# A decoder layer on one core: the bias strip table built from 17 copies, score operands and pool splits ordered behind other DVE work

## The chip, the cores and the metric

The kernel runs on one core of a Trainium2 chip. The time is device microseconds of one execution on that core; smaller is better. The kernel before was timed three times: 660.46, 660.73 and 663.38 us, median 660.73. One more execution was profiled, and all traces here come from it.

## What is computed

One decoder layer over 512 tokens of width 1024, in float32. The parts that matter here are the input projection, the attention branch and the pooling branch:

```python
proj = h @ w_in[l]
q, k, v, p, g = jnp.split(proj, [512, 1024, 1536, 2048], axis=-1)
y_attn = moba_attention(q, k, v, rel_bias) @ w_branch_attn[l]      # 8 heads x 64, causal
y_pool = multiscale_pool(p, w_pool_group[l], pool_scale[l]) @ w_branch_pool[l]
gates = sigmoid(g).reshape(B, S, 2, D)
mixed = gates[:, :, 0] * y_attn + gates[:, :, 1] * y_pool
h = layer_norm(ALPHA * h + mixed @ w_out[l], ln1_g[l], ln1_b[l])
...
```

In the attention a bias `rel_bias[head, bucket(q_pos - k_pos)]` is added to each score, and later keys are masked with -1e30. The bucket is the distance itself up to 15, then grows with its logarithm, to 31 for every distance from 113 on. So along the distances 0 to 511 there are 32 runs of equal buckets: 16 of length 1, then 16 of lengths 2 to 14 and one of 399. The pooling branch takes causal means over windows of 2, 4, 8 and 16 tokens of four groups of 128 channels, and multiplies each group with a small matrix. Behind the part shown follow a gated MLP with a short convolution and a second layer norm; the change does not touch them.

## The kernel before

**Arithmetic.** Each float32 matrix is split into a rounded part `hi` and a rest `lo`; `split` (L65) makes `hi` with one ACT copy and `lo` with one DVE subtraction, and `mm3` (L210) sums three matmuls, hi by hi, hi by lo and lo by hi. Weights come in tiles of 128x1024: a DMA issued by SP into `wraw`, a split into a ring of five `whi`/`wlo` pairs, then the matmuls. `weights(i)` fetches up to three tiles ahead.

**`seven`** (L245) computes two 128-column tiles of a product over all tokens with seven block products in place of eight. It works on four weight combinations: `A` (one tile as it is, loaded as `araw`), `X` (a difference formed in the load: SP writes one tile's part, then POOL adds the other with an accumulating DMA, L163 and L164), `D` (half a tile) and `Y` (formed from `X` and `A` by two DVE additions, L174). The token side uses four combinations `T` made beforehand by `t_form` (L230). Results are put together by ACT copies (L253, L257, L259) and DVE additions: L261, L265, then L266, which writes the first half of the bank in which the last block product, `Y` part 1, goes on. That last block product and the call of `done` are left in `pending` and run inside the next `seven` (or by `flush`), behind its second group of matmuls.

**The order of the start.** The value projection (`v`), two plain pool tiles (`p`, j = 2 and 3), then `seven` for product 0 (pool tiles 0 and 1) and for products 1 to 4 (query tile and key tile of head pairs 0 to 3). `pool_in` (L407) makes window sums with POOL additions (L416) and finishes them on DVE (L419 to L421, and a split into `difs`). `heads_done` (L457) copies a finished query tile to `raw_q` with ACT (L459); for pair 0 it calls `heads(0)` at once.

**`heads(p)`** (L403) makes the score operands of a head pair from `raw_q` and `raw_k`: for each of the two heads one `q` tile (an ACT instruction, L385, and a DVE instruction, L386) and a `k` and a `kl` tile (two ACT, L397, and two DVE, L398). That is six instructions of ACT and six of DVE for a pair. Three buffers each hold the `q`, `k` and `kl` tiles.

**The attention stage.** `scores(h)` (L490) asks for the bias strip of head h+2, multiplies (L501, L502), adds the strip and takes row maxima on DVE (L505), negates them (`nm`, L508), takes exponentials on ACT (L511), and scales on POOL (L516). `trans` transposes on TensorE (L530), `pv` multiplies with the values (L543). The loop over the heads puts one gate tile (`in_tile`, 24 matmuls of 512 columns) into each step. From head 4 on it also splits one of four `zT` tiles, which the pooling half of the branch products reads after the stage.

**The strip table.** Scores of one head need a 128x512 strip whose row shifts by one per partition. POOL builds one row of 640 floats per head in `F_sb` (8 partitions): a memset of the last 128 to -1e30 (L342) and one copy per run of equal buckets from the small table `rel`, 32 copies (L347). A DMA writes the rows to `F_d` in DRAM (L349), and `load_strip` (L351, L353) reads a strip back with overlapping rows. `F_sb` lies in one of the two buffers of the tag `dif`; the strips share three buffers of the tag `strip`, the first of which starts out as `wg_raw`.

**What sets the order.** Every engine runs its instructions in the order that a planner gave them. The planner walks through a simulated execution, and what comes first in the program text has priority among what is ready; work far down in the text is taken early when an engine has nothing else. `tc.issue_after(ins)` makes the instructions of its block come behind `ins` on the engine of `ins`, without waiting for its result.

Of the kernel before, what the change touches and what calls it, by code (L numbers as in the profile page):

```python
# [8 lines left out]
F32 = mybir.dt.float32  # L9
F32R = mybir.dt.float32r  # L10
AF = mybir.ActivationFunctionType
ALU = mybir.AluOpType
PSUM = bass.MemoryType.PSUM

P = 128
S = 512
# [3 lines left out]
H = 8  # L20
# [8 lines left out]
NEG = -1e30  # L29
STRIP = 640  # L30
# [15 lines left out]
def layer_kernel(ctx: ExitStack, tc: tile.TileContext, xT, x, w_v, w_c, rel_bias, invcnt, w_group,  # L46
                 pscale, w_br, w_out, lnr, w_fi, convp, w_fo, out):
    nc = tc.nc
# [16 lines left out]
    def split(hi, lo, src, copy=None):  # L65
        if copy:
            copy(hi, src)
        else:
            nc.scalar.activation(hi, src, AF.Copy)  # L69
        return nc.vector.tensor_tensor(lo, src, hi.bitcast(F32), op=ALU.subtract)  # L70
# [42 lines left out]
    state = {"next": 0, "limit": WO0 - 1}  # L113
# [107 lines left out]
    t1, t2 = slice(0, 256), slice(256, 512)  # L221
# [23 lines left out]
    def seven(key, whole, tt, y, u, done, between=None):  # L245
        ba, bb, bc = (bank(f"s{q}{key[0]}{key[1]}") for q in "abc")
        chain, low, c11 = ba[:, 256:], bb[:, :256], bc[:, :256]

        def b_(k, t):
            return whole[0][:, k, t], whole[1][:, k, t]  # L250

        s_mm(key, "A", 0, b_(k1, t1), chain, True)
        nc.scalar.activation(y, chain, AF.Copy)  # L253
        s_mm(key, "A", 1, b_(k2, t1), c11, True)
        flush()
        s_mm(key, "X", 0, tt["T3"], low, True)
        nc.scalar.activation(u[:, t2], low, AF.Copy)  # L257
        s_mm(key, "Y", 0, tt["nT2"], chain, False)
        nc.scalar.activation(u[:, t1], chain, AF.Copy)  # L259
        s_mm(key, "D", 0, tt["T4"], low, False)  # L260
        nc.vector.tensor_tensor(u[:, t1], u[:, t1], low, op=ALU.add)  # L261
        if between:
            between()
        s_mm(key, "X", 1, tt["nT1"], chain, False, between)
        nc.vector.tensor_tensor(u[:, t2], u[:, t2], chain, op=ALU.add)  # L265
        nc.vector.tensor_tensor(ba[:, t1], y, c11, op=ALU.add)  # L266

        def close():
            s_mm(key, "Y", 1, b_(k2, t2), chain, False, between)
            done(ba, u)  # L270

        pending.append(close)
# [12 lines left out]
    zT = keepp.enter_context(tc.tile_pool(name="keepz", bufs=1)).tile([P, 4, S], F32, name="zT")  # L285
    attn = ExitStack()
    av = attn.enter_context(tc.tile_pool(name="av", bufs=3, side="right", reuse_waits="tile"))
# [5 lines left out]
    ti = {n: tuple(pw.tile([P, 4, 256], F32R, name=f"i{n}_{q}") for q in ("hi", "lo")) for n in parts}  # L293
    pw.tile([P, 48], F32, name="pw_gap2")
    xr = [pw.tile([P, 4, S], F32, name=f"xr{n}") for n in range(2)]
    F_sb = pw.tile([H, STRIP], F32, tag="dif", name="F_sb", bufs=2)

    eps_t = const.tile([P, 1], F32, name="eps_t")
    nc.gpsimd.memset(eps_t, EPS)
# [22 lines left out]
    behind = ExitStack()  # L322
# [16 lines left out]

    behind.close()  # L340
    F_d = dram.tile([H, STRIP], F32, name="F_d")
    nc.gpsimd.memset(F_sb[:, S:], NEG)  # L342
    lo_ = 0
    for b, n in _bucket_runs():
        e = F_sb[:, S - lo_ - n:S - lo_]
        (pst, pn), _ = rel.ap
        nc.gpsimd.tensor_copy(e, bass.AP(tensor=rel.tensor, offset=rel.offset + b, ap=[[pst, pn], [0, n]]))  # L347
        lo_ += n
    nc.gpsimd.dma_start(F_d, F_sb)  # L349

    def load_strip(h):  # L351
        strips[h] = av.tile([P, S], F32, tag="strip", name=f"strip{h}")
        nc.gpsimd.dma_start(strips[h], bass.AP(tensor=F_d.tensor, offset=F_d.offset + h * STRIP,  # L353
                                               ap=[[1, P], [1, S]]))

    load_strip(0)
    load_strip(1)

    vv = av.tile([P, NT, H * DH], F32, name="vv", bufs=1)
    bs = [bank(f"v{j}") for j in range(NT)]  # L360
# [15 lines left out]
    dif = {}  # L376
# [4 lines left out]
    def q_done(p, b):  # L381
        for e in range(2):
            own, oth = slice(e * DH, (e + 1) * DH), slice((1 - e) * DH, (2 - e) * DH)
            t = av.tile([P, S], F32R, tag="q1", name=f"q1_{2 * p + e}")
            nc.scalar.activation(flip(t[own, :]), b[own, :], AF.Copy, scale=DH ** -0.5)  # L385
            nc.vector.scalar_tensor_tensor(flip(t[oth, :]), b[own, :], DH ** -0.5, flip(t[own, :]).bitcast(F32),  # L386
                                           op0=ALU.mult, op1=ALU.subtract)
            Q1[2 * p + e] = t


    def k_done(p, b):
        for e in range(2):
            own, oth = slice(e * DH, (e + 1) * DH), slice((1 - e) * DH, (2 - e) * DH)
            hi = av.tile([P, S], F32R, tag="k1", name=f"k1_{2 * p + e}")
            lo = av.tile([P, S], F32R, tag="kl", name=f"kl_{2 * p + e}")
            for half in (own, oth):
                nc.scalar.activation(hi[half, :], b[own, :], AF.Copy, scale=-1.0)  # L397
                nc.vector.scalar_tensor_tensor(lo[half, :], b[own, :], -1.0, hi[own, :].bitcast(F32),  # L398
                                               op0=ALU.mult, op1=ALU.subtract)
            K1[2 * p + e] = hi  # L400
            KL[2 * p + e] = lo

    def heads(p):  # L403
        q_done(p, raw_q[p])
        k_done(p, raw_k[p])

    def pool_in(j, b, sign=1.0):  # L407
        w = POOL_WINDOWS[j]
# [17 lines left out]
    def pool_out(j):  # L426
        b = bank(f"zb{j}")
        mm3(b, (wg_hi[:, j, :], wg_lo[:, j, :]), dif[j], True, True)
        nc.scalar.activation(zT[:, j, :], b, AF.Copy, scale=psc[:, j:j + 1])
# [20 lines left out]
    raw_q = {}  # L450
# [5 lines left out]

    def heads_done(p, ba):  # L457
        raw_q[p] = av.tile([P, S], F32, tag="rq", name=f"rq{p}")
        nc.scalar.activation(raw_q[p], ba, AF.Copy)  # L459
        if p == 0:  # L460
            heads(0)

    for n in range(1 + pairs):
        if n == 0:
            u, done = xr[1][:, 3, :], pool_done
        else:
            u = raw_k[n - 1] = av.tile([P, S], F32, tag="rk", name=f"rk{n - 1}")
            done = lambda ba, u, p=n - 1: heads_done(p, ba)
        seven(("i", n), (xT_hi, xT_lo), ti, xr[1][:, 2, n % 2 * 256:n % 2 * 256 + 256], u, done)
        if n == 2:  # L470
            for j in PLAIN:
                pool_out(j)
        elif n == 4:
            pool_out(0)
            pool_out(1)
    flush()
# [7 lines left out]
    aw.tile([P, 64], F32, name="aw_gap", bufs=1)  # L484

    Ps = {}
    PTs = {}
    offs = [0, P, 3 * P, 6 * P]

    def scores(h):  # L490
        if h + 2 < H:
            load_strip(h + 2)
        pp = aw.tile([P, 10 * P], F32, tag="pp", name=f"pp{h}")
        nm = aw.tile([P, NT], F32, tag="nm", name=f"nm{h}")
        rs = aw.tile([P, NT], F32, tag="rs", name=f"rs{h}")
        b01 = bank(f"sc{h}_01")
        dst = [b01[:, :2 * P], b01[:, 2 * P:], bank(f"sc{h}_2")[:, :3 * P], bank(f"sc{h}_3")]
        for i in range(NT):
            n = max(2, i + 1) * P
            q = slice(i * P, (i + 1) * P)  # L500
            nc.tensor.matmul(dst[i], Q1[h][:, q], K1[h][:, :n], start=True, stop=False)  # L501
            nc.tensor.matmul(dst[i], Q1[h][:, q], KL[h][:, :n], start=False, stop=True)  # L502
        for i in range(NT):
            n = (i + 1) * P
            nc.vector.tensor_tensor_reduce(out=pp[:, offs[i]:offs[i] + n], in0=dst[i][:, :n],  # L505
                                           in1=strips[h][:, S - n:], scale=1.0, scalar=-3.0e38,
                                           op0=ALU.add, op1=ALU.max, accum_out=nm[:, i:i + 1])
        nc.vector.tensor_scalar(nm, nm, -1.0, None, op0=ALU.mult)  # L508
        for i in range(NT):
            n = (i + 1) * P  # L510
            nc.scalar.activation(pp[:, offs[i]:offs[i] + n], pp[:, offs[i]:offs[i] + n], AF.Exp,  # L511
                                 bias=nm[:, i:i + 1], accum_out=rs[:, i:i + 1])
        nc.vector.reciprocal(rs, rs)
        for i in range(NT):
            n = (i + 1) * P
            nc.gpsimd.tensor_scalar(pp[:, offs[i]:offs[i] + n], pp[:, offs[i]:offs[i] + n], rs[:, i:i + 1], 1.0,  # L516
                                    op0=ALU.mult, op1=ALU.mult)
        Ps[h] = pp
# [30 lines left out]
    scores(1)  # L549
    for h in range(H):  # L550
        if h % 2 == 0 and h + 2 < H:
            heads(h // 2 + 1)
        if h < H - 1:
            in_tile(*fill.pop(0))
        if h + 2 < H:
            scores(h + 2)
        trans(h)
        if h >= 4:
            split(zT_hi[:, h - 4, :], zT_lo[:, h - 4, :], zT[:, h - 4, :])
        if h == H - 1:  # L560
            in_tile(*fill.pop(0))
        if h % 2:
            pv(h // 2)
# [433 lines left out]
def _bucket_runs():  # L997
    b = _bucket_of_dist()
    runs = []
    for v in b:  # L1000
        if runs and runs[-1][0] == v:
            runs[-1][1] += 1
        else:
            runs.append([int(v), 1])
    return runs
# [53 lines left out]
```

## Time and profile before

| what | us |
|---|---|
| timed runs | 660.46, 660.73, 663.38 |
| profiled execution, its own time | 662.12 |
| its span | 660.4 |
| TensorE busy | 638.0 |
| DVE busy | 497.9 |
| ACT busy | 355.0 |
| POOL busy | 133.0 |

The span runs from the first to the last instruction; the profiled execution's time has 1.7 us more around it. Busy time of different engines overlaps. In the timeline a row gives the start in us, the duration in us, the engine, the line, the operation, output and inputs, shapes and a count; in brackets stands how long the engine was idle before and what ended that. PE is TensorE, and its rows of one kind overlap, since matmuls are pipelined. In a view by windows each engine has busy us and a count of instructions; then come the granted clock of TensorE (1.00 is full), the share of the DMA engines and GB/s.

### The profile page before, as it was taken

The numbers are of one execution on the slowest core, as the hardware profiler recorded it, in microseconds if no ns is written. First come the engines' busy times: TensorE is split into PE (matmuls) and PEld (weight loads), VectorE is DVE, ScalarE is ACT, GpSimd is POOL, SyncE is SP. The second block draws the span as 40 slices with busy tenths as digits, with TensorE's granted clock in tenths as the row PEclk, the third lists the DMA queues.
The fourth block names the chain that finished last, engine by engine and source line by source line (L and its number), as shares of the span: only waits on it lengthen the run. The fifth ranks groups of instructions, "written<-read, shape, count | busy, mean of one in ns | idle before, by whom it ended". The sixth has DMA issues, their size and how long they took to land.

```text
span 660.4 us, 10178 instructions
## 1 busy us (share of the span) xinstructions
PE 638.0 (97%) x3910; PEld 566.3 (86%) x3910; DVE 497.9 (75%) x741; ACT 355.0 (54%) x530; POOL 133.0 (20%) x166
## 2 busy tenths in 40 slices
PE   9978997999999999999999999999999999999994
PEld 6868986877778899888998999999999888888884
DVE  6737979864549567939696788888889748799695
ACT  6634858764463555614373555565566436565452
POOL 1945200522214111130001110101100201123302
PEclk9988997999999999999999999999999999999998
DMA  9667434412155743471328668677727974979905
GB/s 330 195 167 175 110 96 128 122 55 65 40 183 139 196 113 104 151 288 35 126 79 218 173 170 191 181 186 181 191 66 260 287 192 106 220 176 199 278 1 127
DMA packets 38016, 104.02 MB, mean 157 GB/s; under 512 B 4040, under 2 KB 4296, under 8 KB 37712
## 3 DMA queue, kind: packets, MB, share of 16 engines
q1 hardware_dynamic: 25280, 69.27, 31.4%
q0 software_dynamic: 12112, 33.06, 25.6%
q10 hardware_dynamic: 576, 1.05, 0.4%
q8 instruction: 30, 0.49, 0.3%
q14 instruction: 18, 0.15, 0.1%
HBM read 100.20 MB, written 3.17 MB: 157 GB/s over the span
## 4 chain that ended last, share of the span: by engine, by line
PE 86%; DVE 4%; POOL 4%; DMA 3%; issue 2%; ACT 1%; SPq 0%; DVEq 0%; POOLq 0%
PE fi L212 4%; PE fi L216 4%; PE fi L215 4%; PE saf L212 4%; PE saf L216 4%; PE saf L215 4%; POOL F_sb L347 3%; PE g L212 2%; PE g L216 2%; PE g L215 2%; PE br L212 2%; PE wo L216 2%; PE br L216 2%; PE br L215 2%; PE wo L215 2%; PE wo L212 2%
## 5 line engine op out<-in xcount | busy, mean ns | idle before, releaser
L70 DVE TENSOR_TENSOR wlo<-wraw,whi 128x1024 fp32r<-128x1024 f32 (+1 forms) x59 | 72.2, 1231 | 18.7 <-ACT whi L69 18.6
L69 ACT ACTIVATE whi<-wraw 128x1024 fp32r<-128x1024 f32 (+1 forms) x58 | 59.6, 1034 | 45.6 <-DMA wraw<-in_w_fo 9.0
L70 DVE TENSOR_TENSOR wlo<-araw,whi 128x1024 fp32r<-128x1024 f32 x46 | 57.8, 1263 | 10.1 <-ACT whi L69 9.4
L69 ACT ACTIVATE whi<-araw 128x1024 fp32r<-128x1024 f32 x46 | 48.2, 1058 | 19.7 <-PE saf L215 6.1
L215 PE MATMUL fi<-hT_lo,whi 128*128 128x512 f32 (+1 forms) x168 | 56.8, 339 | 0.0
L216 PE MATMUL fi<-hT_hi,wlo 128*128 128x512 f32 (+1 forms) x168 | 56.8, 339 | 0.0
L212 PE MATMUL fi<-hT_hi,whi 128*128 128x512 f32 (+1 forms) x168 | 56.5, 340 | 0.0
L164 POOL DMA_DIRECT2D xraw<-in_w_fi x14 | 16.9, 1210 | 163.1 <-DMA xraw<-in_w_fi 90.8
L69 ACT ACTIVATE whi<-tw 128x1024 fp32r<-128x1024 f32 (+1 forms) x30 | 29.4, 983 | 26.2 <-PE fi L215 12.1
L70 DVE TENSOR_TENSOR wlo<-tw,whi 128x1024 fp32r<-128x1024 f32 (+1 forms) x30 | 33.3, 1127 | 9.1 <-ACT whi L69 9.0
L216 PEld LDWEIGHTS fi<-hT_hi,wlo 128*128 128x128 f32 x168 | 31.9, 190 | 3.5
L215 PEld LDWEIGHTS fi<-hT_lo,whi 128*128 128x128 f32 x168 | 31.9, 190 | 3.4
L212 PEld LDWEIGHTS fi<-hT_hi,whi 128*128 128x128 f32 x168 | 31.6, 190 | 3.3
L212 PE MATMUL saf<-hT_hi,whi 128*128 128x256 f32 x112 | 31.7, 283 | 0.0
L215 PE MATMUL saf<-hT_lo,whi 128*128 128x256 f32 x112 | 31.6, 283 | 0.0
L216 PE MATMUL saf<-hT_hi,wlo 128*128 128x256 f32 x112 | 31.5, 283 | 0.0
L212 PE MATMUL sbf<-T_hi,whi 128*128 128x256 f32 x112 | 31.4, 280 | 0.0
L212 PE MATMUL saf<-nT_hi,whi 128*128 128x256 f32 x112 | 31.3, 280 | 0.0
L216 PE MATMUL saf<-nT_hi,wlo 128*128 128x256 f32 x112 | 31.3, 280 | 0.0
L216 PE MATMUL sbf<-T_hi,wlo 128*128 128x256 f32 x112 | 31.3, 279 | 0.0
L215 PE MATMUL sbf<-T_lo,whi 128*128 128x256 f32 x112 | 31.3, 279 | 0.0
L215 PE MATMUL saf<-nT_lo,whi 128*128 128x256 f32 x112 | 31.2, 279 | 0.0
(344 smaller groups left out, 2143.1 us busy)
## 6 DMA issues: line engine op xcount, KB each, us to landing
tw<-in_w_fo POOLq DMA_DIRECT2D x20, 512.0 KB, 7.8
wraw<-in_w_fi SPq DMA_DIRECT2D x16, 512.0 KB, 3.5
araw<-in_w_fi SPq DMA_DIRECT2D x14, 512.0 KB, 4.2
xraw<-in_w_fi SPq DMA_DIRECT2D x14, 512.0 KB, 4.6
xraw<-in_w_fi POOLq DMA_DIRECT2D x14, 512.0 KB, 6.7
wraw<-in_w_c SPq DMA_DIRECT2D x10, 512.0 KB, 3.6
tw<-in_w_fo SPq DMA_DIRECT2D x10, 512.0 KB, 6.2
wraw<-in_w_fo SPq DMA_DIRECT2D x10, 512.0 KB, 8.1
```

Source lines behind the costliest of these rows:

```text
L69: nc.scalar.activation(hi, src, AF.Copy)
L70: return nc.vector.tensor_tensor(lo, src, hi.bitcast(F32), op=ALU.subtract)
L164: nc.gpsimd.dma_start(v, bass.AP(tensor=a.tensor, offset=a.offset, ap=[[pst, pn], [u.offset + S - a.offset, 2], [est, S]]), accum_op=ALU.add)
L212: ins = nc.tensor.matmul(out_, wh, ah, start=start, stop=False, **kw)
L215: nc.tensor.matmul(out_, wh, al, start=False, stop=False, **kw)
L216: nc.tensor.matmul(out_, wl, ah, start=False, stop=stop, **kw)
L347: nc.gpsimd.tensor_copy(e, bass.AP(tensor=rel.tensor, offset=rel.offset + b, ap=[[pst, pn], [0, n]]))
```

## The change

It has three parts.

- The strip table is built in `make_strips`, whose place in the text is behind the second `seven`. The row goes into a buffer of the tag `strip`, the -1e30 columns into another, each with a DMA of its own to `F_d`. Runs of length 1 with consecutive buckets become one copy that reads `rel` backwards: 17 copies in place of 32.
- `heads(0)` is called behind the last `seven` in place of inside `heads_done(0)`, and each `heads` takes instructions behind which its own are held: `heads(0)` behind product 3's L266 on DVE and the `raw_q` copy that is the latest at that place on ACT; `heads(1)` behind product 4's L266 and the last `raw_q` copy; `heads(2)` and `heads(3)` behind the `nm` negation of heads 2 and 4 on DVE.
- The split of a `zT` tile in head h's step is held behind head h's `nm` negation on DVE and its last exponential on ACT.

```diff
-        nc.vector.tensor_tensor(ba[:, t1], y, c11, op=ALU.add)
+        state["add"] = nc.vector.tensor_tensor(ba[:, t1], y, c11, op=ALU.add)
...
-    F_sb = pw.tile([H, STRIP], F32, tag="dif", name="F_sb", bufs=2)
...
-    nc.gpsimd.memset(F_sb[:, S:], NEG)
-    lo_ = 0
-    for b, n in _bucket_runs():
-        e = F_sb[:, S - lo_ - n:S - lo_]
-        (pst, pn), _ = rel.ap
-        nc.gpsimd.tensor_copy(e, bass.AP(tensor=rel.tensor, offset=rel.offset + b, ap=[[pst, pn], [0, n]]))
-        lo_ += n
-    nc.gpsimd.dma_start(F_d, F_sb)
...
-    load_strip(0)
-    load_strip(1)
+    def make_strips():
+        F_sb = av.tile([P, S], F32, tag="strip", name="F_sb")
+        neg = av.tile([P, S], F32, tag="strip", name="neg")
+        nc.gpsimd.memset(neg[:H, :STRIP - S], NEG)
+        (pst, pn), _ = rel.ap
+        runs, lo_ = _bucket_runs(), 0
+        while runs:
+            b, n = runs.pop(0)
+            step = 0
+            if n == 1:
+                while runs and runs[0] == [b + n, 1]:
+                    step, n = -1, n + 1
+                    runs.pop(0)
+            at_ = rel.offset + b - step * (n - 1)
+            nc.gpsimd.tensor_copy(F_sb[:H, S - lo_ - n:S - lo_],
+                                  bass.AP(tensor=rel.tensor, offset=at_, ap=[[pst, pn], [step, n]]))
+            lo_ += n
+        nc.gpsimd.dma_start(F_d[:, :S], F_sb[:H, :])
+        nc.gpsimd.dma_start(F_d[:, S:], neg[:H, :STRIP - S])
+        load_strip(0)
+        load_strip(1)
...
-    def heads(p):
-        q_done(p, raw_q[p])
-        k_done(p, raw_k[p])
+    def heads(p, *behind):
+        with ExitStack() as held:
+            for ins in behind:
+                held.enter_context(tc.issue_after(ins.ins))
+            q_done(p, raw_q[p])
+            k_done(p, raw_k[p])
...
-        nc.scalar.activation(raw_q[p], ba, AF.Copy)
-        if p == 0:
-            heads(0)
+        state["copy"] = nc.scalar.activation(raw_q[p], ba, AF.Copy)
...
-        if n == 2:
+        if n == 1:
+            make_strips()
+        elif n == 2:
             for j in PLAIN:
                 pool_out(j)
+        elif n == 3:
+            hold = [state["add"], state["copy"]]
         elif n == 4:
+            heads(0, *hold)
             pool_out(0)
             pool_out(1)
...
-            heads(h // 2 + 1)
+            heads(h // 2 + 1, *([nms[h]] if h else [state["add"], state["copy"]]))
...
         if h >= 4:
-            split(zT_hi[:, h - 4, :], zT_lo[:, h - 4, :], zT[:, h - 4, :])
+            with tc.issue_after(nms[h].ins), tc.issue_after(exps[h].ins):
+                split(zT_hi[:, h - 4, :], zT_lo[:, h - 4, :], zT[:, h - 4, :])
```

In `scores`, `nms[h]` and `exps[h]` keep head h's `nm` negation and its last exponential.

More of the change, by code (lines that the diff above doesn't have):

```diff
@@ L486, in layer_kernel @@
     Ps = {}
+    nms = {}
+    exps = {}
     PTs = {}
@@ L507, in scores @@
                                            op0=ALU.add, op1=ALU.max, accum_out=nm[:, i:i + 1])
-        nc.vector.tensor_scalar(nm, nm, -1.0, None, op0=ALU.mult)
+        nms[h] = nc.vector.tensor_scalar(nm, nm, -1.0, None, op0=ALU.mult)
         for i in range(NT):
             n = (i + 1) * P
-            nc.scalar.activation(pp[:, offs[i]:offs[i] + n], pp[:, offs[i]:offs[i] + n], AF.Exp,
-                                 bias=nm[:, i:i + 1], accum_out=rs[:, i:i + 1])
+            exps[h] = nc.scalar.activation(pp[:, offs[i]:offs[i] + n], pp[:, offs[i]:offs[i] + n], AF.Exp,
+                                           bias=nm[:, i:i + 1], accum_out=rs[:, i:i + 1])
         nc.vector.reciprocal(rs, rs)
```

## Prediction

> **What bounds the kernel now.** The page first: the span of the profiled execution, and that TensorE is what it is made of. Then the view of who waited for whom, for TensorE over the whole span.
>
> ```profile
> span 660.4 us, 10178 instructions
> ```
>
> ```profile
> PE sai L212 <- DVE sai L266: 6.1, 2, 4.1
> PE sbi L212 <- ACT whi L69: 3.7, 1, 3.7
> PE sai L216 <- DVE wlo L70: 1.3, 1, 1.3
> PE warm_ps L306 <- DVE warm L303: 1.2, 1, 1.2
> PE sbi L216 <- DVE wlo L70: 0.9, 1, 0.9
> ```
>
> Columns: microseconds in total, times, longest. TensorE waits on data about 12 us after its start, all on tiles of the `seven` products of the input projection (`sai`, `sbi`). Nothing from the branch products to the end makes it wait on data, so what is won or lost early reaches the end whole. The timeline of TensorE says where the waits end; bracketed is the idle time in front.
>
> ```profile
> 44.13 0.39 PE L212 MATMUL sbi<-iT_hi,whi 128*128 128x256 f32 x1 [3.73 <-ACT whi L69]
> 59.34 0.58 PE L212 MATMUL sai<-xT_hi,whi 128*128 128x256 f32 x1 [2.03 <-DVE sai L266]
> 84.64 0.39 PE L216 MATMUL sai<-inT_hi,wlo 128*128 128x256 f32 x1 [1.32 <-DVE wlo L70]
> 107.86 0.58 PE L212 MATMUL sai<-xT_hi,whi 128*128 128x256 f32 x1 [4.06 <-DVE sai L266]
> ```
>
> I call them gaps 1 (3.73, and 0.93 close behind), 2, 3 and 4. What follows a gap also costs: busy time and instructions in stretches that begin at a gap's end, with one undisturbed stretch (139.83). PE is the first pair of figures, PEclk the granted clock.
>
> ```profile
> 44.13:51.25 7.12, 6.19 (x37) 5.98 (x38) 7.12 (x11) 5.23 (x9) 0.77 (x1) 0.76 0.58 195
> 59.34:63.58 4.24, 4.24 (x23) 4.24 (x24) 4.17 (x6) 2.93 (x5) 0.09 (x1) 0.60 0.98 197
> 84.64:90.34 5.70, 5.70 (x48) 5.70 (x49) 5.62 (x9) 3.59 (x8) 0.00 (x0) 1.00 0.30 95
> 107.86:110.62 2.76, 2.76 (x13) 2.76 (x14) 2.75 (x12) 0.40 (x2) 0.17 (x1) 0.50 0.40 145
> 110.62:117.67 7.05, 7.05 (x26) 5.64 (x26) 5.04 (x14) 6.77 (x18) 2.35 (x5) 0.77 0.40 121
> 139.83:145.38 5.55, 5.55 (x27) 4.59 (x26) 3.27 (x8) 3.54 (x11) 0.57 (x1) 1.00 0.42 119
> ```
>
> At clock 1.00 a 256-column matmul takes 5.70/48 = 0.119 us. After gap 1 the 37 matmuls should take 4.4 of the 6.19 busy us: 1.8 lost. After gap 2, 4.24 - 23 x 0.119 = 1.5 lost. After gap 3 (1.32 us) nothing, clock 1.00. After gap 4, 2.76 - 13 x 0.119 = 1.2, and the first gate tile takes 7.05 where a later one takes 5.55: together 2.7. So the gaps cost 6.5, 3.5, 1.3 and 6.8, in all 18 us: the most that this change can win.
>
> [...]
>
> **The strip table: fewer copies.** The chain of waits holds the table's building as its one long piece that isn't TensorE's:
>
> ```profile
> 14.46 17.47 POOL F_sb L347 x32
> 32.23 2.25 DMA F_d<-F_sb
> ...
> 36.45 6.49 DMA xr<-in_w_c
> ```
>
> The last row is the accumulating half of the `X` load of product 0: POOL issues it (L164) behind the table's copies, its DMA and three strip loads, in order, and gap 1 waits for it. How long do the 32 copies need, and why? The first row below groups the 16 copies of one element; under it copies beside DVE's instructions.
>
> ```profile
> L347 POOL COPY F_sb<-rel 8x1 f32<-8x1 f32 x16 | 15.1, 997 | 12.9 <-DMA rel<-in_rel_bias 12.9
> ```
>
> ```profile
> 19.14 1.22 DVE L70 TENSOR_TENSOR wlo<-wraw,whi 128x1024 fp32r<-128x1024 f32 x1
> 20.27 1.22 DVE L70 TENSOR_TENSOR inT_lo<-xr,inT_hi 128x1024 fp32r<-128x1024 f32 x1
> 28.30 1.24 DVE L70 TENSOR_TENSOR iT_lo<-xr,iT_hi 128x1024 fp32r<-128x1024 f32 x1
> ```
>
> ```profile
> 19.20 1.19 POOL L347 COPY F_sb<-rel 8x1 f32<-8x1 f32 x1
> 20.34 1.19 POOL L347 COPY F_sb<-rel 8x1 f32<-8x1 f32 x1
> ...
> 31.41 0.51 POOL L347 COPY F_sb<-rel 8x399 f32<-8x399 f32 x1
> ```
>
> A copy starts 0.06 to 0.07 us after each DVE instruction does, and ends with it: one copy per DVE instruction, whatever its size, until DVE falls idle at 28.30 + 1.24 = 29.54. The first 16 take 14.46 + 15.1 = 29.56, exactly that time. The other 16 then run in 31.92 - 29.54 = 2.4 us. The change folds the 16 single copies into one with a step of -1 and keeps 16: seventeen. Sixteen of these meet the same busy DVE, and the seventeenth (the 0.51 us one) starts at about 29.54 and ends at 30.05. So the saving is 31.92 - 30.05 = **1.9 us**, not the 15 x 0.997 = 15 us that the mean suggests.
>
> [...]
>
> Does the 1.9 arrive? Three rows of the DMA side:
>
> ```profile
> 24.92 0.89 SPq L163 DMA_DIRECT2D xr<-in_w_c  x2
> ```
>
> ```profile
> xr<-in_w_c SPq DMA_DIRECT2D x2, 512.0 KB, 5.1
> ```
>
> ```profile
> 34.78 1.69 POOL L353 DMA_DIRECT2D strip<-F_d  x3 [1.79 <-DMA F_d<-F_sb]
> ```
>
> The accumulation adds to what SP loads at 24.92, which lands 5.1 later, at 30.0; POOL came to it at 36.45. So 36.45 - 30.0 = 6.4 is the most that any shortening in front of it can give. Strip 2, which the text asks for much later, stands in front of it too: the planner takes what is ready, and the later place of `make_strips` in the text should not move the copies. The new write of the NEG columns is one more POOL DMA; its data are ready at the start, and it costs nothing there. If it queues behind the first write's landing, it costs another 2.25 + 0.76: net -1.1. Bounds -1.1 to 6.4; I take **1.9**. It reaches the end of gap 2, since DVE works without a break from this load on until it waits for POOL's window sums, which follow the same load.
>
> **The held score operands.** What `heads` puts on DVE now, and the rows it displaces:
>
> ```profile
> 72.30 2.77 DVE L398 SCALAR_TENSOR_TENSOR kl<-rk,k 64x512 fp32r<-64x512 f32 x4
> ...
> 80.38 1.41 DVE L386 SCALAR_TENSOR_TENSOR q<-rq,q 64x512 fp32r<-64x512 f32 x2
> ...
> 83.36 1.22 DVE L70 TENSOR_TENSOR wlo<-araw,whi 128x1024 fp32r<-128x1024 f32 x1
> ...
> 99.40 1.23 DVE L70 TENSOR_TENSOR wlo<-wraw,whi 128x1024 fp32r<-128x1024 f32 x1 [4.42 <-ACT whi L69]
> ...
> 104.62 0.42 DVE L265 TENSOR_TENSOR rk<-rk,sai 128x256 f32<-128x256 f32 x1
> 104.96 1.22 DVE L70 TENSOR_TENSOR wlo<-wraw,whi 128x1024 fp32r<-128x1024 f32 x1
> 106.09 1.38 DVE L398 SCALAR_TENSOR_TENSOR kl<-rk,k 64x512 fp32r<-64x512 f32 x2
> 107.39 0.41 DVE L266 TENSOR_TENSOR sai<-xr,sci 128x256 f32<-128x256 f32 x1
> ```
>
> *Gap 3.* `heads(0)` (six DVE instructions, 2.77 + 1.41 = 4.2 us) goes behind product 3's L266. The `wlo` at 83.36 that gap 3 waits for has 4.2 us less in front of it. Between 0 (another operand is late) and 1.32; I take **1.3**, as the relief is three times the gap. The 4.2 us fit into DVE's idle 4.42 in front of 99.40; without that cover they would come on top of the work before product 4's L266.
>
> *Gap 4.* L266 at 107.39 comes after L265, a `wlo` and two `kl`; the `kl` and the `q` around them are of later heads, which the change puts behind this L266 and behind the last `raw_q` copy on ACT. At best L265 and L266 stand alone and the gap is 0.83: gain 4.06 - 0.83 + 2.7 = 5.9. If the `wlo` stays between, 2.05, which costs clock as gap 2 did: 4.06 - 2.05 + 2.7 - 1.5 = 3.2. Nothing, if `heads(0)` lands there. I take **4.5**, the middle of the first two.
>
> *The new wait.* All of `heads(1)` now follows the `raw_q` copy; the scores of head 2 and their exponentials come behind it. Rows of ACT, the copy and the last of the exponentials of heads 0 and 1 behind it, and the mean of a `k` instruction:
>
> ```profile
> 111.58 0.58 ACT L459 ACTIVATE rq<-sai 128x512 f32<-128x512 f32 x1
> ...
> 118.00 0.19 ACT L511 ACTIVATION_READ_ACCUMULATOR pp<-pp,nm 128x1 f32 x1
> ```
>
> ```profile
> L397 ACT ACTIVATE k<-rk 64x512 fp32r<-64x512 f32 x6 | 3.8, 629 | 0.8 <-PE sc L501 0.7
> ```
>
> Head 2 needs four ACT instructions (2.5) and one more on DVE (0.69). Straight behind the copy that is ready at 112.2 + 3.2 = 115.4; behind all exponentials at 118.2 + 3.2 = 121.4. TensorE ends gate tile 0 at 110.62 + 5.55 = 116.2. The wait is 0 to 5.2, with up to 2.7 of clock behind it. Another gate tile (5.55) can go first, so I take **1.0**. The z splits (0.69 each on DVE) are needed only by the branch products; eight heads lie before that: nothing, and at most 2.8 if all four come last.
>
> **Sum.** 1.9 + 1.3 + 4.5 - 1.0 = 6.7 us. The profiled execution took 662.12 (1.7 around its span): 655.4. The median of the three runs, 660.73, is 1.39 below it, so I forecast **654.0**, with 650 to 657.4 as its own range.
>
> **Rivals.** *The loads overtake the strips* (0.19): `make_strips` stands behind two `seven` in the text, so the accumulating loads may get POOL first. Then the chain gains its full 6.4, and with 1.3 and 5.9, nothing lost, it is 13.6: 647.1. Against it: strip 2 already runs ahead of them. *The wait moves* (0.20): scores of head 2 wait the full 5.2: 1.9 + 1.3 + 4.5 - 5.2 = 2.5, so 658.2; for it speaks ACT's unbroken work from 111.58 on. *The holds become the bound* (0.16): each of the three held pairs is late by its six DVE instructions, 6 x 0.69 = 4.1: 7.7 - 12.4 = -4.7, **665.4**. It decides as soon as a pair's operands end later than the gate tile in front of its scores; against it, DVE is busy only 3.27 of 5.55 us at 139.83. The forecast keeps 0.45.
>
> **Chances.** Half a per cent (3.3 us) is about what a measurement tells from no change. Faster by more: 0.41 of the forecast, 0.19, and 0.07 of the moved wait: 0.67. Within: 0.04, 0.12 and 0.02: 0.18. Slower: 0.15. The range runs from beyond the first rival, 645, to 663, short of the last.
>
> **What would show it.** Right: 17 copies that start one per DVE instruction and end near 30; the accumulating load near 34.5; gap 1 shorter by some 1.9 and gap 2 still there; no wait at product 2's `wlo`; gap 4 under 2.1 and the gate tile behind it nearer 5.55; `sc` without an idle in front. Wrong: POOL's loads ahead of the strips, copies at 0.12 us each under a busy DVE, gap 4 still 4 us with `heads(0)` in front of L266, or a new wait at `sc`.

## The result, and the profile after

The changed kernel takes 666.61 us (median of 7 runs, 664.50 to 667.20) beside 661.37 for the kernel before (7 runs on the same chips): ratio 1.0072, 95% interval 1.0054 to 1.0090. It is slower by 0.7%, where 654.0 was forecast, and outside the range of 645 to 663. The profiled execution took 666.64, 1.7 us around its span.

The view of who waited for whom, TensorE, over the whole span of the changed kernel (us in total, times, longest):

```profile
PE tr L549 <- POOL pp L535: 5.9, 3, 5.0
PE sbi L212 <- ACT whi L69: 2.4, 1, 2.4
PE sai L212 <- ACT whi L69: 2.2, 1, 2.2
PE sc L521 <- DVE kl L409: 1.4, 2, 1.2
PE sai L212 <- DVE sai L266: 1.3, 1, 1.3
```

The four gaps of before are there or gone as follows: gap 1 is 2.4 (and 0.7 for `wlo`), gap 2 is 2.2, now for `whi`, gap 3 is gone, gap 4 is 1.3. New is the first row: the transposes `tr` wait for POOL's `pp`, the scaled probabilities of head 0, by far the longest wait of the execution. The timeline of TensorE around it:

```profile
105.21 0.39 PE L212 MATMUL sai<-xT_hi,whi 128*128 128x256 f32 x1 [1.27 <-DVE sai L266]
...
114.07 0.39 PE L521 MATMUL sc<-kl,q 128*128 128x256 f32 x1 [1.19 <-DVE kl L409]
...
120.10 0.47 PE L549 MATMUL tr<-ident,pp 128*128 128x128 f32 x1 [4.99 <-POOL pp L535]
121.08 0.69 PE L549 MATMUL tr<-ident,pp 128*128 128x128 f32 x2 [0.51 <-POOL pp L535]
```

And TensorE by windows (PE busy and count first, the granted clock in front of the last two figures):

```profile
106.73:112.30 5.57, 5.57 (x27) 4.61 (x26) 5.51 (x20) 5.29 (x9) 1.18 (x2) 1.00 0.67 215
112.20:115.20 3.00, 1.72 (x9) 0.95 (x7) 2.91 (x6) 2.96 (x4) 0.00 (x0) 1.00 0.63 206
120.10:123.00 2.90, 1.98 (x7) 1.29 (x8) 2.82 (x4) 2.84 (x8) 2.90 (x3) 0.50 0.75 220
122.76:128.60 5.84, 5.84 (x23) 4.72 (x22) 2.89 (x6) 2.10 (x9) 5.84 (x9) 0.75 0.01 2
```

Gate tile 0 starts 3.9 us earlier than before (106.73 against 110.59) and runs at full clock, 5.57 us in place of 7.05. Then TensorE waits 1.2 and 5.9 us, and the clock falls to 0.50 and 0.75 behind the wait. Why the probabilities are late stands on ACT and POOL:

```profile
107.82 0.58 ACT L473 ACTIVATE rq<-sai 128x512 f32<-128x512 f32 x1
108.30 1.27 ACT L396 ACTIVATE q<-rq 64x512 fp32r<-64x512 f32 x2
109.60 2.60 ACT L408 ACTIVATE k<-rk 64x512 fp32r<-64x512 f32 x4
112.22 0.63 ACT L396 ACTIVATE q<-rq 64x512 fp32r<-64x512 f32 x1
112.76 1.25 ACT L408 ACTIVATE k<-rk 64x512 fp32r<-64x512 f32 x2
114.02 1.28 ACT L530 ACT_TABLE_LOAD   x1
115.31 0.40 ACT L530 ACTIVATE pp<-pp,nm 128x128 f32<-128x128 f32 x1
```

```profile
118.10 0.54 POOL L344 DMA_DIRECT2D strip<-F_d  x1 [7.35 <-DVE rs L532]
118.67 3.46 POOL L535 TENSOR_SCALAR pp<-pp,rs 128x128 f32<-128x128 f32 x3
```

Behind the last `raw_q` copy ACT makes all operands of heads 2 and 3 and those of head 4 (5.7 us), then loads a table in the exponentials' line (1.28 us), and only at 115.31 takes head 0's first exponential. TensorE has been ready for head 0's transposes since 115.1. The same place in the kernel before, on ACT, POOL and TensorE:

```profile
112.17 1.28 ACT L511 ACT_TABLE_LOAD   x1
113.72 0.40 ACT L511 ACTIVATE pp<-pp,nm 128x128 f32<-128x128 f32 x1 [0.26 <-DVE nm L508]
```

```profile
116.33 2.08 POOL L516 TENSOR_SCALAR pp<-pp,rs 128x128 f32<-128x128 f32 x4 [3.66 <-DVE rs L513]
```

```profile
118.93 0.82 PE L530 MATMUL tr<-ident,pp 128*128 128x128 f32 x6
```

Count from the last `raw_q` copy, at 111.58 before and 107.82 after. TensorE comes to head 0's transposes 7.3 us behind it in both (118.93 and 115.11). The first exponential starts 2.1 us behind it before and 7.5 us after. POOL's scaling is slower too: four instructions took 2.08 us before, three take 3.46 now.

### The profile page after: what moved, and what is told of

It reads as the page before. It is cut to its first block, busy times and chain, and to the rows that moved or that the text cites. A ratio compares the mean times of both kernels' runs of the same rounds, so it can differ in the third digit from the quotient of the medians.

```text
span 664.9 us, 10168 instructions
## 1 busy us (share of the span) xinstructions
PE 639.9 (96%) x3910; PEld 566.2 (85%) x3910; DVE 501.9 (75%) x741; ACT 354.9 (53%) x530; POOL 132.9 (20%) x152
## 4 chain that ended last, share of the span: by engine, by line
PE 83%; issue 8%; POOL 4%; DMA 3%; DVE 2%; SPq 0%; ACT 0%; DVEq 0%; POOLq 0%; ACTq 0%
PE fi L212 4%; PE fi L215 4%; PE fi L216 4%; PE saf L212 4%; PE saf L216 4%; PE saf L215 4%; PE br L212 2%; POOL F_sb L361 2%; PE br L215 2%; PE wo L212 2%; PE wo L216 2%; PE br L216 2%; PE wo L215 2%; PE g L212 2%; PE g L216 2%
```

## The experiments

Fifteen kernels' profiles can be laid side by side at three marks, the first gate tile, the first output-projection matmul (`wo`) and the end. From `wo` to the end all take 389.2 to 389.8 us, so the first two tell the whole difference between these executions. Each row is one execution, and those of one kernel scatter by 1 to 5 us: the profiled ones of e10 and e12 were 1.7 and 1.5 us faster than their medians.

| kernel | first gate tile | first wo | between | span |
|---|---|---|---|---|
| before | 110.59 | 271.19 | 160.6 | 660.4 |
| after | 106.73 | 275.67 | 168.9 | 664.9 |
| e1_strips | 109.18 | 277.40 | 168.2 | 666.7 |
| e2_holds | 103.75 | 272.20 | 168.5 | 662.0 |
| e3_heads1_free | 110.24 | 270.47 | 160.2 | 659.7 |
| e4_exp_first | 108.17 | 276.35 | 168.2 | 665.6 |
| e5_two_tiles | 107.94 | 272.74 | 164.8 | 662.0 |
| e6_holds_two_tiles | 104.25 | 269.24 | 165.0 | 658.5 |
| e7_before_two_tiles | 109.47 | 273.73 | 164.3 | 663.0 |
| e8_strips_last | 100.04 | 268.55 | 168.5 | 658.3 |
| e9_strips_last_tiles | 101.22 | 261.33 | 160.1 | 650.6 |
| e10_tiles_mid | 104.38 | 264.47 | 160.1 | 653.7 |
| e11_before_strips_last | 103.70 | 273.18 | 169.5 | 662.4 |
| e12_before_tiles_mid | 108.19 | 267.18 | 159.0 | 656.4 |
| e13_holds_tiles_mid | 104.22 | 264.32 | 160.1 | 653.6 |

Ratios below are to the kernel before on the same chip, with the 95% interval.

**e1: the strip part alone.** `heads(0)` back in `heads_done`, nothing held:

```diff
-        elif n == 3:
-            hold = [state["add"], state["copy"]]
         elif n == 4:
-            heads(0, *hold)
...
-            heads(h // 2 + 1, *([nms[h]] if h else [state["add"], state["copy"]]))
+            heads(h // 2 + 1)
...
-            with tc.issue_after(nms[h].ins), tc.issue_after(exps[h].ins):
-                split(zT_hi[:, h - 4, :], zT_lo[:, h - 4, :], zT[:, h - 4, :])
+            split(zT_hi[:, h - 4, :], zT_lo[:, h - 4, :], zT[:, h - 4, :])
```

> Only the strip table's part of the change: 17 copies in buffers of their own; heads and z splits as before. Theory A (the loss is made by the held score operands, whose ACT instructions run ahead of the exponentials of heads 0 and 1): no wait at tr, gap 4 near 4 us as before, the copies still one per DVE instruction and done near 29.5; the time within 2 us of the kernel before, 659 to 663. Theory B (the loss comes from the strip part, through a new order of POOL and DVE work around 48 to 60 us): 664 or more, with gap 2 as long as after the change.

668.34 us, ratio 1.0099 (1.0071 to 1.0127). Theory A falls in its plain form: nothing is held here, and the same wait is there.

```profile
PE tr L548 <- POOL pp L534: 6.6, 1, 6.6
PE sbi L212 <- ACT whi L69: 3.9, 1, 3.9
```

But it does not come about in the same way. Gap 4 fell to 2.1 us by the new order alone, and the planner put a weight split in front of the exponentials on ACT:

```profile
114.62 1.06 ACT L69 ACTIVATE whi<-wraw 128x1024 fp32r<-128x1024 f32 x1 [3.29 <-PE g L215]
115.90 1.28 ACT L408 ACTIVATE k<-rk 64x512 fp32r<-64x512 f32 x2 [0.22 <-PE sc L519]
```

ACT waits 3.3 us for TensorE's gate tile there, then makes operands of a later head, and head 0's first exponential comes at 119.15. Theory B had the time right and the place wrong: gap 2 is 3.2 us, but from the first gate tile on 7.6 us more are lost.

**e2: the holds alone**, with the strip table of before; the order of the holds is left as changed:

```diff
+    F_sb = pw.tile([H, STRIP], F32, tag="dif", name="F_sb", bufs=2)
...
+    for b, n in _bucket_runs():
+        e = F_sb[:, S - lo_ - n:S - lo_]
...
-    def make_strips():
...
-        if n == 1:
-            make_strips()
-        elif n == 2:
+        if n == 2:
```

> Only the holds of the score operands and the z splits; the strip table as before with 32 copies. Theory A: waits at sc and tr of 6 to 7 us together near 112 to 122, product 2's wlo wait gone, gap 4 below 2 us; 664 to 669. Theory B: no loss, 655 to 660.

663.91 us, ratio 1.0052 (1.0033 to 1.0070), a hair under what theory A expected. In the places it is as theory A had it: `tr` waits 5.5, `sc` 1.6, product 2's `wlo` wait is gone, gap 4 is 1.3. So each part alone makes the kernel slower, and TensorE waits in the same place; on ACT the held operands are in front of the exponentials here, as in the changed kernel, and the weight split in e1.

**e3: heads(1) free.**

```diff
-            heads(h // 2 + 1, *([nms[h]] if h else [state["add"], state["copy"]]))
+            heads(h // 2 + 1, *([nms[h]] if h else []))
```

> The changed kernel with one hold undone: heads(1) is free, heads(0), heads(2), heads(3) and the z splits stay held. Theory A: the exponentials of heads 0 and 1 start about 4 to 5 us earlier after the raw_q copy, the wait at tr falls from 5.9 us to under 1, and about 5 to 9 us come back: 658 to 662. Theory B: as the changed kernel, 665 to 668.

662.22 us, ratio 1.0023 (1.0007 to 1.0039), just above what theory A expected. No wait at `tr`, and 160.2 between the marks. But gap 4 is back (2.2 us, after 1.5 at `sc`), and the first gate tile starts at 110.24 and needs 6.9 us. What was gained in the stage had not been won in front of it.

**e4: the exponentials first on ACT.**

```diff
-            heads(h // 2 + 1, *([nms[h]] if h else [state["add"], state["copy"]]))
+            heads(h // 2 + 1, *([nms[h]] if h else [state["add"], exps[1]]))
```

> The changed kernel with heads(1) still held, but on ACT behind head 1's last exponential in place of the last raw_q copy. Theory A: the exponentials follow the raw_q copy at once, tr no longer waits, TensorE takes a second gate tile before the scores of head 2: 655 to 661, unless the scores of head 2 come late instead (then a wait at sc of 3 to 5 us and 662 to 666). Theory B: as the changed kernel, 665 to 668.

665.35 us, ratio 1.0067 (1.0041 to 1.0093). The wait at `tr` goes, and one comes in front of the scores of head 2, longer than the 3 to 5 us expected for that case:

```profile
PE sc L520 <- ACT k L408: 7.4, 1, 7.4
```

With gap 4 closed, ACT has both jobs behind the `raw_q` copy, and whichever comes second is late. This gave theory C: TensorE arrives too early for what ACT, DVE and POOL can have ready, and needs other work there, in either order of ACT.

**e5, e6, e7: one more gate tile in front**, on the changed kernel, on the holds alone and on the kernel before; head 6's step gives its tile up, and the last stays at the end.

```diff
-        if h < H - 1:
+        for _ in range((2, 1, 1, 1, 1, 1, 0, 0)[h]):
             in_tile(*fill.pop(0))
```

> The changed kernel with its gate tiles one step earlier: two in front of the scores of head 2, none in head 6's step. Theory C (closing gap 4 brings TensorE to head 0's transposes before its softmax is done, so the same time is waited there, in whatever order ACT works): the second gate tile, 5.6 us, covers the wait at tr; from the start of the first gate tile to the first branch matmul 76 to 79 us in place of 85, and 657 to 661 in all. Theory A (the held operands themselves are too slow for the stage): the wait goes on to the next heads, 664 to 668.

> The holds without the strip part, with the gate tiles one step earlier as in the run beside it. Theory C: the wait at tr of 5.5 us and most of the 1.4 us at sc go, 76 to 79 us for the stage, 654 to 658: faster than the kernel before. Theory A: 662 to 666.

> The kernel before with nothing but the gate tiles one step earlier. Theory C: there is no wait at tr to cover here, since gap 4 has already given head 0's softmax its time, and gap 4 stays near 4 us: within 1.5 us of the kernel before. If the earlier tiles are good by themselves: 655 to 658.

661.72 (1.0025; 1.0008 to 1.0043), 660.67 (1.0017; 1.0003 to 1.0030) and 664.16 us (1.0063; 1.0048 to 1.0079). The wait of 5 us went, to 1.0, in e5 and e6. But e7 shows a price that I had not expected: near 177 us the transposes, and then the first branch product, wait where the tile is missing. To the first branch product e5 takes 77.0 us and e6 77.2, as expected, but to the first `wo` 164.8 and 165.0, over 4 us more than before. e5's time was just above what theory C expected, e6's too high, e7's too: the tile seems to have been taken from a step that needed it.

```profile
PE tr L530 <- POOL pp L516: 1.5, 1, 1.5
...
PE br L212 <- ACT oT_hi L69: 1.2, 1, 1.2
```

**e8: the strip loads last.** On the changed kernel, each strip load held on POOL behind product 1's accumulating load:

```diff
+            added[key] = nc.gpsimd.dma_start(v, ..., accum_op=ALU.add)
...
+        with tc.issue_after(added["i", 1].ins):
             nc.gpsimd.dma_start(strips[h], ...)
```

> The changed kernel with all strip loads held behind product 1's accumulating load on POOL. Theory D (the strip part gains nothing because the table's write and the strip loads share the DMA engines with the X and D loads just then): POOL comes to product 0's accumulating load near 30.5 in place of 33.8 to 37, it lands near 37, gap 1 falls below 1.5 us, gap 2 ends 4 to 6 us earlier, the wait at tr stays: 659 to 663. [...]

660.27 us, ratio 1.0005 (0.9996 to 1.0014): by the ratios some 4.4 us better than the changed kernel, and 6.6 us between the two profiled spans, all of it early. The rows are the first accumulating loads on POOL and the DVE addition that waits for the first of them:

```profile
31.00 2.53 POOL L165 DMA_DIRECT2D xr<-in_w_c  x2 [1.07 <-DMA xr<-in_w_c]
32.75 2.46 POOL L346 DMA_DIRECT2D strip<-F_d  x3
```

```profile
37.77 1.36 DVE L175 TENSOR_TENSOR araw<-xr,araw 128x512 f32<-128x512 f32 x1 [7.56 <-DMA xr<-in_w_c]
```

Gap 1 is gone altogether, and the first gate tile starts at 100.04, 6.7 us earlier than in the changed kernel and 10.5 earlier than before. The stage stays as long as in the changed kernel, 168.5 us (5.1 of waits at `tr`, 1.5 at `sc`).

The load is used at 37.77 in place of 42.49, 4.7 us earlier, and 3.5 of these are POOL's: it comes to the load at 31.00 in place of 34.49, since the strip loads no longer stand in front. That the rest comes of theory D's shared DMA engines is not shown. From POOL's start to the use the load took 5.9 to 6.8 us in the three kernels with the strip loads behind it (e8, e9, e11). It took 7.9 to 8.0 us in three that have them in front and whose POOL came to it at 33.7 to 34.5 (the changed kernel, e3, e10).

**e9 and e10: the tile from the middle.** Head 3's step gives its tile up, on e8 and on the changed kernel:

```diff
-        if h < H - 1:
+        for _ in range((2, 1, 1, 0, 1, 1, 1, 0)[h]):
             in_tile(*fill.pop(0))
```

> The changed kernel with the strip loads behind product 1's accumulating load (as in e8_strips_last) and one gate tile moved from head 3's step to the front, so that two stand before the scores of head 2 and the last one stays at the end. Theory C: e8's early start of the first gate tile (100 us) is kept, and from there to the first output-projection matmul it takes about 161 to 163 us in place of 169.6, with no wait of over 1 us at tr: 650 to 655, faster than both kernels. Rival (the stage cannot be run faster than head by head, the wait only moves on to head 3's or a later step): 657 to 661.

> The changed kernel with the same move of one gate tile from head 3's step to the front and nothing else. Theory C: the first gate tile starts at 107 to 108 us as after the change, from there to the output projection 161 to 163 us in place of 169: 658 to 661, 6 to 8 us better than the changed kernel. Rival: 663 or more.

e9: 651.93 us, ratio 0.9874 (0.9855 to 0.9893); e10: 657.17, ratio 0.9947 (0.9930 to 0.9963). Both take 160.1 us between the marks, with ACT's operands still in front of the exponentials; theory C holds, and e9 beats both kernels. (The 169.6 us named in the expectation is 168.5 by the row of the first `wo`.) The longest of TensorE's waits of e9:

```profile
PE sai L213 <- DVE sai L267: 3.8, 2, 2.5
PE warm_ps L306 <- DVE warm L303: 1.2, 1, 1.2
PE tr L551 <- POOL pp L537: 0.9, 1, 0.9
PE sbi L217 <- DVE wlo L70: 0.4, 1, 0.4
```

**e11: the strip loads last, on the kernel before** (32 copies, nothing held on DVE):

```diff
     def load_strip(h):
...
-        nc.gpsimd.dma_start(strips[h], ...)
+        with tc.issue_after(added["i", 1].ins):
+            nc.gpsimd.dma_start(strips[h], ...)
-    load_strip(0)
-    load_strip(1)
...
+        if n == 1:
+            load_strip(0)
+            load_strip(1)
-        if n == 2:
+        elif n == 2:
```

> The kernel before (32 copies, nothing held on DVE) with its strip loads behind product 1's accumulating load. Theory D (the strip loads in front of the accumulating loads cost the early gaps, whatever the number of copies): POOL comes to the accumulating load about 1.9 us later than in e8_strips_last, near 33; gap 1 falls below 2 us and gap 2 ends 3 to 4 us earlier. If gap 4 stays (about 4 us) head 0's softmax has its time, and the whole gain arrives: 655 to 658. If the new order closes gap 4, the wait at tr takes it back: 659 to 662.

663.26 us, ratio 1.0047 (1.0030 to 1.0064). POOL came to the accumulating load at 33.03, and gap 1 is 2.0. The new order closed gap 4 to 2.1, and `tr` waits 6.1: the second branch of what was expected, and somewhat worse. On ACT it is as in e1: a weight split waits 4.9 us for the gate tile, and the first exponential starts at 115.01, 10 us behind the `raw_q` copy.

**e12 and e13: the tile from the middle, on the kernel before and on the holds alone,** with the edit of e9.

> The kernel before with only the move of head 3's gate tile to the front. Theory C: gap 4 (about 4 us) still gives head 0's softmax its time, so there is nothing at tr to cover: within 1.5 us of the kernel before, 659 to 662. Rival (the move is good by itself): 652 to 656.

> The holds with the move of the gate tile, the strip table as before with 32 copies. It stands beside e10_tiles_mid, which has the strip part too, and so prices the strip part where nothing later takes it back. If the strip part gains its 1.9 us: 659 to 660. If it gains nothing, since the table's write lands late among the X and D loads: as e10, 656 to 658. If it costs: 653 to 656.

e12: 659.63, ratio 0.9983 (0.9972 to 0.9994); e13: 655.10, ratio 0.9915 (0.9900 to 0.9930). The move alone is worth 1.1 us: gap 4 is still 4.1 us, the exponentials start 2.5 us behind the `raw_q` copy, and there is no wait at `tr` to cover. With the wait covered, the holds are worth 0.9983 - 0.9915, some 4.5 us, give or take 1.3. And e10, which has the strip part too, is 0.3% (0.7 to 3.6 us) slower than e13, on another chip; their intervals touch, and the two profiled spans are equal (653.7 and 653.6). So the strip part gains nothing here, and whether it costs anything stays open. No run tests the holds of the last two pairs or the z splits alone.

## Why the prediction was wrong, by its own steps

**The copies: right.** The changed kernel's row of the copies, and DVE's last instruction of that stretch:

```profile
14.62 14.60 POOL L361 COPY F_sb<-rel 8x16 f32<-8x16 f32 x17 [12.00 <-DMA rel<-in_rel_bias]
```

```profile
29.08 1.22 DVE L70 TENSOR_TENSOR iT_lo<-xr,iT_hi 128x1024 fp32r<-128x1024 f32 x1 [0.63 <-ACT iT_hi L69]
```

Seventeen copies of 2 to 399 elements take 14.6 us, as sixteen of one element took 15.1 before: one per DVE instruction, with a median of 1.19 us beside DVE's 1.22. They end at 29.22, as the last of them could run in DVE's gap of 0.63; 30.05 was forecast.

**What the strip part is worth: mis-sized, 1.9 forecast, nothing measured.** The chain of waits of the changed kernel, in order of time (start, us):

```profile
29.52 2.76 DMA F_d<-F_sb
...
34.49 7.98 DMA xr<-in_w_c
...
42.49 0.70 DVE araw L174
```

POOL came to the accumulating load at 34.49, as forecast (34.5). But the load needed 7.98 us in place of 6.49 and was used at 42.49, 0.47 earlier than before. The table's write now falls into a busier stretch (the share of the DMA engines is 0.66 to 0.77 from 29 to 33 us, while the write of before lay mostly in the 0.13 from 33 to 35) and lands after 2.76 us in place of 2.25. I had moved two DMA steps at their old durations. One execution each is thin evidence, so take all kernels with the strip loads in front. In the six with the new table the write took 1.9 to 4.4 us, POOL came to the load at 33.7 to 37.0, and the load was used at 41.7 to 43.7. In the six with the old table these are 2.1 to 2.7, 35.3 to 36.7 and 42.6 to 43.4. Where POOL came earlier the load took longer. e8 shows that the place of the strip loads, not the number of copies, held the larger sum: the cap of 6.4 that I had named for the first rival (POOL at 31.0, 30.0 worked out).

**Gap 3: right**, 1.3 gained; no wait is left at product 2's `wlo`. **Gap 4: right**, 1.27 with full clock behind it; 4.06 - 1.27 + 2.7 = 5.5 against 4.5. e13 beside e12 measures both together at 4.5 us in the time, where 1.3 + 4.5 was forecast.

**The new wait: the step that failed.** The sum had 1.0 there, at the scores of head 2, with bounds of 0 and 5.2 and up to 2.7 of clock. TensorE waited 1.2 there and 5.9 us at head 0's transposes. The stage between the marks took 8.3 us longer, and 1.5 more were hidden in it, since its first tile ran faster: 9.8 in place of 1.0. Without this step the start would have stood: 5.4 us were won by the end of the first gate tile (112.20 for 117.64), and 5.4 - 9.8 = -4.4 is about the 4.5 us by which the span grew. Two things were missing. I asked whether the scores of head 2 would be ready, but not whether head 0's softmax would, and it stands on the same ACT queue. And I counted on another gate tile to go first: the planner's order puts the transposes of head 0 in front of it, as it did before. In the kernel before, ACT had made operands in front of the last `raw_q` copy (rows of `k` and `q` up to 106.2 us), partly beside gap 4, and the softmax followed the copy at once. The holds moved that work behind the copy, in front of the softmax, which then started 5.4 us later behind the copy while TensorE came no later. So gap 4 had been time for operands that now cost the same again; to close it was worth nothing until other work of TensorE stood there.

**The rivals.** "The wait moves" came nearest in its mechanism, 658.2 for the scores of head 2, with the target and the clock loss missing. "The holds become the bound" came nearest in its number, 665.4, by luck: it priced three pairs at 4.1 us each, and only the first was late, by 1.2 us at its scores. "The loads overtake the strips" did not happen by itself; e8 made it happen.

**The clock.** The prediction charged 1.5 us of clock for a gap of about 2 us, from the one row of gap 2. The runs do not bear that out as a rule. Two views of the 3 us behind gap 2, of the kernel before (a gap of 2.03 us) and of e12 (2.10 us, in the same place):

```profile
59.34:62.34 3.00, 3.00 (x14) 3.00 (x15) 2.97 (x4) 1.69 (x4) 0.09 (x1) 0.50 0.91 188
```

```profile
58.77:61.77 3.00, 3.00 (x25) 3.00 (x26) 2.97 (x4) 2.84 (x5) 0.29 (x2) 1.00 0.91 173
```

Matmuls of 256 columns also came 0.12 us apart, as at clock 1.00, after 2.00 (e11) and 2.07 us (e1); after 1.92 (e5) they came 0.21 us apart from 62.80 on, 1.6 us behind the end of the gap. So in these runs a gap of 1.9 to 2.1 us may cost clock or not; what decides it is not shown. After the 4.06 us of gap 4 in the kernel before and the 4.99 us at `tr` in the changed kernel the clock was 0.50. Behind the 4.06 us of e7 and e12 and the 6.08 us of e11 matmuls of 512 columns came 0.43 us apart, where those of the changed kernel's gate tile 0 came every 0.23 us at clock 1.00.

## What to carry to other kernels

A wait that ends on a late operand also gives time to whatever runs beside it, and work that is moved out of its way lands in front of something else. Before closing one, follow every other input that TensorE needs next, engine by engine, and name the work that will stand there in its place; here one gate tile moved forward turned a loss of 0.7% into a gain of 0.5%, and with the strip loads behind the weight loads into 1.3%. And a small transfer that is moved earlier must be priced in its new company: here its landing took between 1.9 and 4.4 us among the loads beside it.

## What the runs showed beyond that

POOL's copies kept the pace of a busy DVE (sixteen of one element took 15.1 us before, the sixteen others 2.4 with DVE idle), and in these rows DVE takes longer beside POOL. They are a DVE addition of the changed kernel and its like of before; in the changed kernel it starts just before one of POOL's window sums and needs 2.55 us:

```profile
50.19 2.55 DVE L174 TENSOR_TENSOR araw<-araw 128x512 f32<-128x512 f32 x1
```

```profile
49.75 0.69 DVE L174 TENSOR_TENSOR araw<-araw 128x512 f32<-128x512 f32 x1
```

```profile
50.67 1.52 POOL L430 TENSOR_TENSOR pw<-pt 128x527 f32<-128x527 f32 x1
```

It ends at 50.19 + 2.55 = 52.74, that is 0.55 us after this sum (50.67 + 1.52 = 52.19). The kernel before has the like: a `difs` subtraction that starts at 51.49, just behind the start of a window sum (51.25 + 1.52 = 52.77), needs 1.84 us and ends 0.56 us after it; in the changed kernel the same subtraction, with no sum beside it, needs 0.69. What holds DVE up there is not shown: no run here tests it, and the slow addition starts 0.48 us before the sum. And a change of the text in one place moved the planner's order in others: e1 and e11 hold no operand, and in both gap 4 halved and the exponentials came late.
